# A two-layer decoder trunk: the expert stage written as a stream of 24 steps, the residual added once a token

## The chip, the core and the metric

The kernel runs on one core of a Trainium2 chip. Its engines are TensorE (PE in the profile; PEld is its loading of stationary operands), VectorE (DVE), ScalarE (ACT), GpSimd (POOL) and SyncE (SP), which here only issues transfers. The metric is the device time of one execution in microseconds.

## The reference, cut to what matters

512 tokens of width 1024 pass two layers. Each layer is a mixer (gated spatial mixing in the first, dilated attention in the second, memory attention in both), a layer norm, and an expert stage with a second layer norm:

```python
x = layer_norm(ALPHA * x + att, ln1_g, ln1_b)
expert, gate = route(x, w_router, b_router)          # 2 of 16 experts a token
ffn = sum over the token's 2 experts of
      gate * ((silu(x @ w_gate[e]) * (x @ w_up[e])) @ w_down[e])
x = layer_norm(ALPHA * x + ffn, ln2_g, ln2_b)        # LN_EPS = 1e-5
```

ALPHA is 4 to the power 1/4. The weights of an expert are three matrices of 1024 x 1024 in fp32, 12.6 MB, and each of the 2 x 16 experts is computed.

## The kernel before, in words

A product of fp32 operands is made from three matmuls: each operand is split into a high part (fp32r, made on ScalarE by a copy) and a low part (raw minus high, made on VectorE); `mm3` (L119) issues high x high, high x low and low x high. `split_to` (L115) makes the two parts, and a weight tile of 128 x 1024 is one split (L116, L117, tiles `wh` and `wl`; four `wh`, and three `wl` in layer 0 or four in layer 1, by `lows`).

`moe` (L1148) is the expert stage of a layer. `route` (L842) has given each token two experts and a rank in each; `index` and `slots` (L915, L1007) turn ranks into lists of token rows by a one-hot on VectorE (L1003) and small matmuls on TensorE, and, from expert 2 on, for two experts at a time. `gather` (L1044) fetches an expert's up to 128 rows from `hbuf` in HBM with an indirect transfer on GpSimd's queue. `turn` (L1049) transposes them on TensorE into `xh` and `xl`, and then ScalarE scales the gathered rows in place by a factor that holds ALPHA for the token's first expert and 0 for its second (L1054). `gate_up` (L1061) makes, in two halves of 512 columns, the gate and the up product (tiles `pg`, `pu`; four splits and 24 matmuls each), the silu on ScalarE, `sg` = silu x gate factor x up on VectorE (L1077), four transposes (`at`, L1080), and its parts `ah` and `al` (L1083, L1084). `down` (L1106) makes the down product (`pd`) in two halves; ScalarE copies it to `y`, GpSimd adds the scaled rows (`y <- y, xg`, L1130), and an indirect transfer scatters `y` into `ybuf` (L1131), which holds two rows a token. So the residual travels with the first expert's rows. An expert is 24 splits of weights, 144 matmuls, and 16 transposes.

The last expert isn't scattered: its rows stay on the chip (`yl`) and `last_slots` (L1087) makes a one-hot `oT` for it. `combine` (L1255) then adds, for each of the four tiles of 128 tokens, the two rows of `ybuf` (`yrows`, loaded by `load_rows`, L495), where the factor `far` blanks the row that the last expert would have filled (one ScalarE and one VectorE operation a tile), and the last expert's rows by matmuls with `oT`, and takes the norm. Its order on VectorE is written by hand as a string of steps (L575, L1316).

Weights arrive in loads of 2 MB into a ring of eight slots (`load_half`, L1139), issued by SP in one batch an expert; a load waits until the slot's last reader is done. Ahead of the experts stand `gates` (L928), `extra` (L960), `first_factors` (L1034: one-hots and small matmuls for experts 0 and 1), the split of two weight tiles, and `overflow` (L1197): every engine reads from `tabi` the number of blocks beyond 128 rows an expert and branches over a loop that does them. No such block occurs here.

The order of instructions on an engine in the expert stage is the program's scheduler's, apart from places that name an instruction to be behind (`issue_after`). `InOrder` (L58) wraps an engine so that each of its instructions is put behind the one before:

```python
with self.tc.issue_after(self.prev) if self.prev and self.strict else ExitStack():
    r = getattr(self.eng, name)(*args, **kw)
self.prev = r.ins
```

Of the kernel before, what the change touches and what calls it, by code (L numbers as in the profile page):

```python
# [38 lines left out]
SKIP = 4096  # L39
GUESS = 0xDF0259DF - (1 << 32)  # L40
# [33 lines left out]
class Trunk:  # L74
    def __init__(self, ctx, tc, a):
        self.tc, self.nc, self.a = tc, tc.nc, a
        self.lows = 3
# [5 lines left out]
        self.xbuf = tc.dram_tile([S, D], F32, name="xbuf")  # L83
        self.obuf = tc.dram_tile([2, S, 264], F32, name="obuf")
# [26 lines left out]
    def parts_tiles(self, pool, bufs):  # L111
        return (pool.tile([P, 1024], F32R, tag="wh", name="wh", bufs=bufs),
                pool.tile([P, 1024], F32R, tag="wl", name="wl", bufs=min(bufs, self.lows)))

    def split_to(self, raw, hi, lo, eng=None):  # L115
        self.hi = self.nc.scalar.activation(hi, raw, AF.Copy)  # L116
        self.sub = (eng or self.nc.vector).tensor_sub(lo, raw, hi.bitcast(F32))  # L117
# [53 lines left out]
    def rsqrt_steps(self, t, var, dve):  # L171
# [3 lines left out]
        yield dve.tensor_scalar(v, var, EPS, None, op0=OP.add)  # L175
# [11 lines left out]
    def norm_steps(self, pool, z, zn, dve, act):  # L187
# [6 lines left out]
        yield from self.rsqrt_steps(mv[:, 2:5], mv[:, 1:2], dve)  # L194
# [74 lines left out]


    def rows_to_T(self, rows, hi, lo, bank=None, order=(), act=()):

        nc = self.nc
        for b in range(2):
            x = (bank or self.tp)("xt")
            for i in range(4):
                nc.tensor.transpose(x[:, i * P:(i + 1) * P], rows[:, (4 * b + i) * P:(4 * b + i + 1) * P], self.ident)  # L277
            x3 = x.rearrange("p (a b) -> p a b", a=4)
            with ExitStack() as es:
                for ins in act:  # L280
                    es.enter_context(self.tc.issue_after(ins))
                nc.scalar.activation(hi[:, 4 * b:4 * b + 4], x3, AF.Copy)  # L282
            with ExitStack() as es:
                for ins in order:
                    es.enter_context(self.tc.issue_after(ins))
                nc.vector.tensor_sub(lo[:, 4 * b:4 * b + 4], x3, hi[:, 4 * b:4 * b + 4].bitcast(F32))


    def layer_a(self):
# [20 lines left out]
        with ExitStack() as em:  # L310
# [59 lines left out]
            for t in range(NT):  # L370
                nc.gpsimd.dma_start(self.ybuf[2 * t * P:2 * (t + 1) * P].rearrange("(p k) d -> p (k d)", k=2), zero)
# [123 lines left out]
    def load_rows(self):  # L495

        self.ys = [v[:, i * 2048:(i + 1) * 2048].rearrange("p (k d) -> p k d", k=2)
                   for v in (self.slot("yrows") for _ in range(2)) for i in range(2)]
        for t in range(NT):
            self.nc.sync.dma_start(self.ys[t], self.ybuf.rearrange("(t p k) d -> t p k d", p=P, k=2)[t])  # L500

    def layer_b(self):
# [3 lines left out]
        with ExitStack() as em:  # L506
# [72 lines left out]
            load(0)  # L579
            qT = pb.tile([P, 2, S], F32, name="qTb")  # L580
# [261 lines left out]
    def route(self, pl, lg):  # L842
# [65 lines left out]
        self.at, self.fac = [], []  # L908
        for e in range(2):
            self.index(pl, e, 1, "f", S - 1)  # L910
# [4 lines left out]
    def index(self, pool, e0, n, tag, mask=None):  # L915

        ix = self.keep(f"ix{e0}", [P, 2, n], I32)
        info = self.info if mask else self.all6
# [88 lines left out]
    def slots(self, pool, rank, info, n, ix, fac, tag, mask=None):  # L1007
# [17 lines left out]
        if fac is not None:  # L1025
            self.reduce_factors(fac, v[:, :, 2:])
# [79 lines left out]
    def down(self, act, xg, ix, i, weights, split, nodep=None, inplace=False):  # L1106
# [20 lines left out]
        if last:  # L1127
            return
# [251 lines left out]
```

## Time and profile before

| | us |
|---|---|
| median of three runs | 1726.21 (1724.07 to 1726.26) |
| the profiled execution | 1723.48 |
| its span, first to last instruction | 1721.6 |
| TensorE's mean granted clock | 0.968 |
| experts of layer 0 | from 229.1 to 810.8 |
| experts of layer 1 | from 1103.5 to 1686.8 |

Times of the trace count from the start of the span. Between the two expert stages lie the combine of layer 0 and the mixer of layer 1; behind the second lies the combine of layer 1. In a row of the trace an arrow out<-in names what is written and read, `xN` counts instructions, and a bracket [idle <-releaser] gives how long the engine had stood before and what ended that.

### The profile page before, as it was taken

What the parts mean: (1) busy time and instruction counts of PE and PEld (TensorE: products, weight loads), DVE (VectorE), ACT (ScalarE), POOL (GpSimd) and SP (SyncE); (2) the same over time, 40 slices, a digit from 0 to 9 for tenths busy, and PEclk for the clock granted to TensorE, in tenths of its full rate; (3) what the DMA queues carried; (4) which work ended last, traced back from release to release, by engine and by line L of the source; (5) the groups of instructions that cost most, each with busy time, mean ns of one, the idle gap of its engine ahead of it and who ended that gap; (6) DMA issues with size and microseconds to landing.
All of it is one profiled execution on the core that took longest, in us unless ns stands there. A gap on an engine that the chain in (4) does not pass through costs nothing. (4 is left out here: it accounts for less than half of the span.)

```text
span 1721.6 us, 21239 instructions
## 1 busy us (share of the span) xinstructions
PE 1603.4 (93%) x7608; PEld 1270.8 (74%) x7608; DVE 1441.0 (84%) x1910; ACT 1176.0 (68%) x1487; POOL 303.2 (18%) x170
## 2 busy tenths in 40 slices
PE   7999799999999999999799998499999999999994
PEld 6778577777777777777677777377777787877773
DVE  3856789999999998998735457899999999998997
ACT  3644467878888887886434434488887888888873
POOL 1201511332111211111300002211112111121002
PEclk9999889999999999999899997699999999999997
DMA  7516589999999999985422244589998999999951
GB/s 313 214 49 245 196 319 356 351 349 371 356 369 369 361 374 365 352 311 211 147 98 74 95 175 145 196 340 362 347 352 337 368 377 377 368 349 363 360 199 49
DMA packets 50739, 486.93 MB, mean 283 GB/s; under 512 B 9973, under 2 KB 10101, under 8 KB 21056
## 3 DMA queue, kind: packets, MB, share of 16 engines
q1 hardware_dynamic: 39408, 453.63, 67.8%
q0 software_dynamic: 10640, 29.75, 4.6%
q10 hardware_dynamic: 576, 2.10, 0.4%
q8 instruction: 62, 1.02, 0.2%
q14 instruction: 53, 0.43, 0.1%
HBM read 471.47 MB, written 29.39 MB: 291 GB/s over the span
## 5 line engine op out<-in xcount | busy, mean ns | idle before, releaser
L117 DVE TENSOR_TENSOR wl<-wexp,wh 128x1024 fp32r<-128x1024 f32 x768 | 945.9, 1271 | 50.1 <-ACT wh L116 30.0
L116 ACT ACTIVATE wh<-wexp 128x1024 fp32r<-128x1024 f32 x768 | 802.7, 1060 | 163.2 <-PE pg L123 73.5
L1130 POOL TENSOR_TENSOR y<-y,xg 128x1024 f32<-128x1024 f32 x30 | 92.4, 3080 | 837.9 <-ACT y L1126 837.9
L122 PE MATMUL pg<-wl,xh 128*128 128x512 f32 x512 | 205.6, 401 | 8.8 <-DVE wl L117 7.8
L122 PE MATMUL pd<-wl,ah 128*128 128x512 f32 x512 | 205.7, 402 | 5.6 <-DVE wl L117 4.6
L121 PE MATMUL pd<-wh,ah 128*128 128x512 f32 x512 | 206.5, 403 | 0.0
L123 PE MATMUL pd<-wh,al 128*128 128x512 f32 x512 | 204.4, 399 | 0.0
L123 PE MATMUL pg<-wh,xl 128*128 128x512 f32 x512 | 203.0, 396 | 0.0
L121 PE MATMUL pg<-wh,xh 128*128 128x512 f32 x512 | 202.6, 396 | 0.3 <-ACT xh L282 0.3
L122 PE MATMUL pu<-wl,xh 128*128 128x512 f32 x512 | 199.7, 390 | 1.0 <-DVE wl L117 1.0
L123 PE MATMUL pu<-wh,xl 128*128 128x512 f32 x512 | 199.5, 390 | 0.0
L121 PE MATMUL pu<-wh,xh 128*128 128x512 f32 x512 | 199.3, 389 | 0.0
L122 PEld LDWEIGHTS pg<-wl,xh 128*128 128x128 f32 x512 | 96.8, 189 | 43.5 <-DVE wl L117 24.6
L122 PEld LDWEIGHTS pd<-wl,ah 128*128 128x128 f32 x512 | 96.3, 188 | 32.2 <-DVE wl L117 12.0
L121 PEld LDWEIGHTS pd<-wh,ah 128*128 128x128 f32 x512 | 96.3, 188 | 25.3 <-ACT wh L116 5.1
L122 PEld LDWEIGHTS pu<-wl,xh 128*128 128x128 f32 x512 | 96.1, 188 | 22.3 <-DVE wl L117 2.2
L123 PEld LDWEIGHTS pd<-wh,al 128*128 128x128 f32 x512 | 96.2, 188 | 21.9 <-DVE al L1084 1.8
L121 PEld LDWEIGHTS pg<-wh,xh 128*128 128x128 f32 x512 | 96.9, 189 | 20.1 <-ACT xh L282 0.8
L121 PEld LDWEIGHTS pu<-wh,xh 128*128 128x128 f32 x512 | 96.1, 188 | 20.4
L123 PEld LDWEIGHTS pg<-wh,xl 128*128 128x128 f32 x512 | 96.6, 189 | 19.5 <-issue 0.9
L123 PEld LDWEIGHTS pu<-wh,xl 128*128 128x128 f32 x512 | 96.1, 188 | 19.9
L1046 POOL DMA_INDIRECT xg<-hbuf,ix x32 | 58.6, 1830 | 84.6 <-ACT ah L1083 67.7
(397 smaller groups left out, 2402.3 us busy)
## 6 DMA issues: line engine op xcount, KB each, us to landing
wexp<-w_moe SPq DMA_DIRECT2D x177, 2048.0 KB, 8.8
wexp<-w_moe SPq DMA_DIRECT2D x24, 1024.0 KB, 6.8
yrows<-ybuf SPq DMA_DIRECT2D x8, 1024.0 KB, 7.6
wb<-wbr SPq DMA_DIRECT2D x4, 2048.0 KB, 11.0
wexp<-w_moe POOLq DMA_DIRECT2D x3, 2048.0 KB, 10.7
ybuf<-mematt POOLq DMA_DIRECT2D x4, 1024.0 KB, 14.1
wina<-wina SPq DMA_DIRECT2D x2, 2048.0 KB, 18.7
wouta<-w_out_a SPq DMA_DIRECT2D x2, 2048.0 KB, 10.9
```

Source lines behind the costliest of these rows:

```text
L116: self.hi = self.nc.scalar.activation(hi, raw, AF.Copy)
L117: self.sub = (eng or self.nc.vector).tensor_sub(lo, raw, hi.bitcast(F32))
L121: nc.tensor.matmul(out, a[0], b[0], start=start, stop=False)
L122: nc.tensor.matmul(out, a[0], b[1], start=False, stop=False)
L123: self.mm = nc.tensor.matmul(out, a[1], b[0], start=False, stop=stop)
L1046: return self.nc.gpsimd.indirect_dma_start(out=xg, out_offset=None, in_=self.hbuf, in_offset=off, bounds_check=S - 1, oob_is_err=False)
L1130: nc.gpsimd.tensor_add(y, y, xg)
```

## The change

The expert stage is written as a stream. `mm3` takes an order; in the expert stage it is high x high, low x high, high x low, so the low part of the weights comes last. `block` goes through an expert in 24 steps, one split weight tile and six matmuls each, and calls `part` before and `at` behind each step's products; VectorE, ScalarE and TensorE are wrapped with `InOrder` for the length of the stage, so they run in the order in which the program writes. The high part is written four steps ahead of its use and the low part three (five `wh`, four `wl`). The `sg` product of a half comes ahead of the split in steps 8 and 16, its transposes behind the products of these steps, and its parts in steps 9 and 17. Index lists are made for one expert at a time in steps 10 to 13; the next rows are transposed in steps 17 to 20, and the gather of the expert after the next goes out in step 13. SP issues one load every four steps.

The residual no longer travels with the rows. The gate is divided by ALPHA and the norm's epsilon by its square, so that x is added unscaled, once a token: in the last expert's steps 10 to 17 SP fetches the four tiles of `hbuf`, and GpSimd adds to the first row of each token in `ybuf` (already loaded) first x and then the second row. `far` and its operations go, `ybuf` is zeroed for both layers (in layer B by four copies on GpSimd's queue from a zero buffer of 1 MB, `zbuf`, which layer A writes). The factors of experts 0 and 1 are made in their steps 0 to 5, behind the branch; three weight tiles are split ahead of it instead of two.

```diff
+AHEAD_H, AHEAD_L = 4, 3
+READY = 3
...
-    def mm3(self, out, a, b, start, stop):
-        nc = self.nc
-        nc.tensor.matmul(out, a[0], b[0], start=start, stop=False)
-        nc.tensor.matmul(out, a[0], b[1], start=False, stop=False)
-        self.mm = nc.tensor.matmul(out, a[1], b[0], start=False, stop=stop)
+    def mm3(self, out, a, b, start, stop, order=((0, 0), (0, 1), (1, 0))):
+        for n, (i, j) in enumerate(order):
+            self.mm = self.pe.matmul(out, a[i], b[j], start=start and n == 0, stop=stop and n == 2)
...
-            for t in range(NT):
-                nc.gpsimd.dma_start(self.ybuf[2 * t * P:2 * (t + 1) * P].rearrange("(p k) d -> p (k d)", k=2), zero)
+            for rows in [self.ybuf[2 * t * P:2 * (t + 1) * P] for t in range(NT)] + [self.zbuf]:
+                nc.gpsimd.dma_start(rows.rearrange("(p k) d -> p (k d)", k=2), zero)
...
             load(1)
             load(0)
+            for t in range(NT):
+                nc.gpsimd.dma_start(self.ybuf[2 * t * P:2 * (t + 1) * P], self.zbuf)
...
+    def block(self, pool, x, fac, part, y, at):
...
+        for c in range(24):
+            i, j = divmod(c, 4)
+            key = [("pg", 0), ("pu", 0), ("pg", 1), ("pu", 1), ("pd", 0), ("pd", 1)][i]
+            if j == 0:
+                bank[key] = self.acc(key[0])
+            if c in (8, 16):
+                times(c // 8 - 1)
+            if c == 17:
+                list(turns.pop(1))
+            if c == 20:
+                y(0, bank["pd", 0])
+            p = part(c)
+            if c in (4, 12):
+                silu(c // 8)
+            if c == 9:
+                list(turns.pop(0))
+            self.products(bank[key], x if i < 4 else a, p, j)
+            if c in (8, 16):
+                half = c // 8 - 1
+                turns[half] = self.turn(sg[half], self.tp("at"), a, half)
+                next(turns[half])
+            at(c)
+        y(1, bank["pd", 1])
...
+        self.dve, self.act, self.pe = (InOrder(tc, e, True) for e in (nc.vector, nc.scalar, nc.tensor))
...
+            if e == 0:
+                spread((0, 1, 2), index(0))
+                spread((3, 4, 5), index(1))
+            if e + 2 < NE:
+                spread((10, 12, 13), index(e + 2))
+            if not last:
+                spread((17, 18, 18, 18, 19, 19, 20), rows_in(e + 1))
+            else:
+                spread((11, 12, 13), self.last_slots(pool))
+                for t in range(NT):
+                    do(10 + t, lambda t=t: self.presum(t, 0))
+                for t in range(NT):
+                    do(14 + t, lambda t=t: self.presum(t, 1))
+
+            def get(c, e=e):
+                k = 24 * e + c
+                while len(his) < min(k + AHEAD_H + 1, 24 * NE):
+                    his.append(self.wh_tile(pool))
+                    self.hi = self.act.activation(his[-1], chunk(len(his) - 1), AF.Copy)
+                while len(los) < min(k + AHEAD_L + 1, 24 * NE):
+                    n = len(los)
+                    los.append(self.wl_tile(pool))
+                    self.sub = self.dve.tensor_sub(los[n], chunk(n), his[n].bitcast(F32))
+                return his[k], los[k]
+
+            def at(c, e=e, jobs=jobs):
+                for job in jobs.get(c, ()):
+                    job()
+                if c % 4 == 3:
+                    n = 6 * e + c // 4 + 8
+                    if n < 6 * NE:
+                        loaded.append(self.load_half(layer, *divmod(n, 6), 2 if n >= 6 * (NE - 1) else 1))
+                    elif n < 6 * NE + 4:
+                        self.tail_slot(layer, n - 6 * NE)
+
+            def y(half, bank, e=e, last=last):
+                s = slice(half * 512, (half + 1) * 512)
+                if last:
+                    self.split_to(bank, self.yl[0][:, s], self.yl[1][:, s])
+                    return
+                if half == 0:
+                    ys[e] = self.y_tile()
+                self.act.activation(ys[e][:, s], bank, AF.Copy)
+                if half:
+                    self.scatter(ys.pop(e), self.at[e], scat)
...
+    def presum(self, t, i):
+        y = self.ys[t]
+        if i == 0:
+            r = self.y_tile() if t == 2 else self.xg[t % 2 if t < 2 else 0]
+            self.nc.sync.dma_start(r, self.hbuf[t * P:(t + 1) * P, :])
+        self.nc.gpsimd.tensor_add(y[:, 0], y[:, 0], y[:, 1] if i else r)
...
             y = [self.ys[t][:, i] for i in range(2)]
-            act.activation(y[0], y[0], AF.Copy, scale=self.far[:, t, 0:1])
-            dve.scalar_tensor_tensor(y[0], y[1], self.far[:, t, 1:2], y[0], op0=OP.mult, op1=OP.add)
...
-            steps["b", t] = steps["c", t] = self.norm_steps(pool, z, y[0], dve, act)
+            steps["b", t] = steps["c", t] = self.norm_steps(pool, z, y[0], dve, act, EPS / ALPHA ** 2)
```

## Rows read from the trace of the kernel before

**Rows 1.** The page, part 1: busy us, share of span, instructions.

```profile
PE 1603.4 (93%) x7608; PEld 1270.8 (74%) x7608; DVE 1441.0 (84%) x1910; ACT 1176.0 (68%) x1487; POOL 303.2 (18%) x170
```

**Rows 2.** By stage: stretch, us, busy us by engine, clock, DMA share, GB/s.

```profile
229.00:776.00 547.00, 537.27 (x2461) 427.48 (x2462) 513.20 (x500) 446.89 (x496) 101.03 (x42) 1.00 0.91 356
812.00:1103.00 291.00, 247.20 (x1299) 194.08 (x1300) 178.62 (x464) 113.07 (x261) 45.97 (x37) 0.89 0.34 124
1434.00:1470.00 36.00, 35.95 (x163) 28.73 (x163) 33.75 (x32) 30.04 (x34) 6.17 (x3) 1.00 0.95 378
1688.00:1722.00 34.00, 12.74 (x32) 6.75 (x32) 27.16 (x65) 8.96 (x12) 10.09 (x4) 0.73 0.16 62
```

**Rows 3.** Timeline, TensorE: first products of experts (start us, us, engine, line, operation).

```profile
266.87 0.47 PE L121 MATMUL pg<-wh,xh 128*128 128x512 f32 x1
...
775.99 0.39 PE L121 MATMUL pg<-wh,xh 128*128 128x512 f32 x1
...
1140.71 0.47 PE L121 MATMUL pg<-wh,xh 128*128 128x512 f32 x1
...
1469.59 0.39 PE L121 MATMUL pg<-wh,xh 128*128 128x512 f32 x1
...
1505.04 0.40 PE L121 MATMUL pg<-wh,xh 128*128 128x512 f32 x1
...
1652.05 0.40 PE L121 MATMUL pg<-wh,xh 128*128 128x512 f32 x1
```

**Rows 4.** Waits of TensorE's weight loads, 267 to 776 us (total, times, longest).

```profile
PEld pg L122 <- DVE wl L117: 10.6, 19, 1.4
PEld at L1080 <- DVE sg L1077: 8.4, 19, 1.1
```

**Rows 5.** Groups by line, 267 to 776 us (count, busy, mean ns, idle before).

```profile
L117 DVE TENSOR_TENSOR wl<-wexp,wh 128x1024 fp32r<-128x1024 f32 x337 | 420.7, 1287 | 17.1 <-ACT wh L116 6.8 <-issue 2.7 <-PE pd L122 2.3
...
L1077 DVE SCALAR_TENSOR_TENSOR sg<-sg,fac,pu 128x512 f32<-128x512 f32 x28 | 20.8, 742 | 10.7 <-PE pu L123 10.7
L1084 DVE TENSOR_TENSOR al<-at,ah 128x512 fp32r<-128x512 f32 x28 | 19.1, 683 | 0.5 <-ACT ah L1083 0.5
```

**Rows 6.** All operations on the low parts, whole span (min/median/max ns).

```profile
L117 DVE TENSOR_TENSOR wl<-wexp,wh x768: 1208/1218/3433, 221.4 to 1683.6; 128x1024 fp32r<-128x1024 f32 x192
```

**Rows 7.** Timeline of VectorE around an add of GpSimd, layer 0.

```profile
303.36 2.35 DVE L117 TENSOR_TENSOR wl<-wexp,wh 128x1024 fp32r<-128x1024 f32 x2
...
306.23 7.97 DVE L117 TENSOR_TENSOR wl<-wexp,wh 128x1024 fp32r<-128x1024 f32 x5
```

**Rows 8.** Timeline of GpSimd in the same stretch.

```profile
305.09 6.89 POOL L1130 TENSOR_TENSOR y<-y,xg 128x1024 f32<-128x1024 f32 x1 [29.82 <-ACT y L1126]
```

**Rows 9.** All operations on the expert's rows (min/median/max ns).

```profile
L1130 POOL TENSOR_TENSOR y<-y,xg x30: 2507/2636/6890, 267.5 to 1652.9; 128x1024 f32<-128x1024 f32 x30
```

**Rows 10.** Groups by line, 1140 to 1652 us: the one-hot.

```profile
L1003 DVE TENSOR_TENSOR so<-rk,slot 128x512 bf16<-128x512 f32 x11 | 7.5, 685 | 0.0
```

**Rows 11.** Timeline of VectorE ahead of layer 1's experts: the overflow count.

```profile
1092.09 0.14 DVE L970 CAST tabi<-tab 1x1 int32<-1x1 f32 x1
```

**Rows 12.** Timeline of TensorE ahead of layer 1's experts.

```profile
1095.13 0.36 PE L1041 MATMUL fac<-all,so 128*128 128x4 bf16 x8 [5.07 <-DVE all L955]
1101.66 1.94 PE L277 MATMUL xt<-ident,xg 128*128 128x128 f32 x8 [6.17 <-PEq L1201]
```

**Rows 13.** Timeline of TensorE ahead of layer 0's experts.

```profile
227.75 1.07 PE L277 MATMUL xt<-ident,xg 128*128 128x128 f32 x8 [1.92 <-DVEq L1201]
```

**Rows 14.** Transfers in 40 slices of 740 to 812 us, mean GB/s.

```profile
GB/s 396 378 118 378 407 369 364 382 401 309 428 428 405 410 396 46 93 198 0 0 0 0 0 87 36 305 432 428 428 428 391 346 410 423 437 428 437 36 0 0
```

**Rows 15.** Operations with the factor far, both layers (min/median/max ns).

```profile
L67 DVE SCALAR_TENSOR_TENSOR yrows<-yrows,far x8: 1237/1280/2468, 811.4 to 1698.4; 128x1024 f32<-128x1024 f32 x8
```

**Rows 16.** Waits in the first 80 us.

```profile
ACT wh L116 <- DMA wina<-wina: 2.2, 3, 1.8
```

**Rows 17.** Waits of SP's queue, 229 to 776 us (total, times, longest).

```profile
SPq L1144 <- DVE wl L117: 498.5, 88, 9.7
```

More of the change, by code (lines that the diff above doesn't have):

```diff
@@ L493, in load_branch @@
         self.nc.sync.dma_start(qk, self.a["wbr"][:, c:c + 4096])
[L495 to L500, printed above, removed]
     def layer_b(self):
@@ L1087, in last_slots, with scatter @@
-    def last_slots(self, pool, layer):
-        nc = self.nc
-        self.hgb = self.slot("ln2")
-        self.load_ln2(layer, 0)
-        y2 = self.slot("ylast").bitcast(F32R)
-        self.yl = y2[:, :D], y2[:, D:2 * D]
-        self.oT = y2[:, 2 * D:2 * D + S]
-        so = self.one_hot(pool, self.rk[:, :, NE - 1:])
-        x = self.tp("oT")
-        for t in range(NT):
-            nc.tensor.matmul(x[:, t * P:(t + 1) * P], so[:, t], self.identb, start=True, stop=True)
-        nc.scalar.activation(self.oT, x, AF.Copy)
+    def scatter(self, y, ix, nodep):
+        st = self.nc.gpsimd.indirect_dma_start(out=self.ybuf, out_offset=bass.IndirectOffsetOnAxis(ap=ix[:, 1], axis=0),
+                                               in_=y, in_offset=None, bounds_check=2 * S - 1, oob_is_err=False)
+        for other in nodep:
+            self.tc.declare_no_dep(st.ins, other.ins, reason="rows of other tokens")
+        nodep.append(st)
@@ L1146, in load_half, with wh_tile, wl_tile, turn @@
         return t
+    def wh_tile(self, pool):
+        return pool.tile([P, 1024], F32R, tag="wh", name="wh", bufs=AHEAD_H + 1)
+    def wl_tile(self, pool):
+        return pool.tile([P, 1024], F32R, tag="wl", name="wl", bufs=AHEAD_L + 1)
+    def turn(self, src, bank, parts, half):
+        for q in range(4):
+            self.pe.transpose(bank[:, q * P:(q + 1) * P], src[:, q * P:(q + 1) * P], self.ident)
+        s = slice(4 * half, 4 * half + 4)
+        x3 = bank.rearrange("p (a b) -> p a b", a=4)
+        yield
+        self.act.activation(parts[0][:, s], x3, AF.Copy)
+        yield
+        self.dve.tensor_sub(parts[1][:, s], x3, parts[0][:, s].bitcast(F32))
@@ new lines, in y_tile, with two, products @@
+    def y_tile(self):
+        return self.px.tile([P, D], F32, tag="y", name="y", bufs=1)
+    def two(self, pool, names):
+        return [pool.tile([P, KT, P], F32R, tag=n, name=n, bufs=1) for n in names]
+    def products(self, bank, a, part, j):
+        h, l = part
+        for q in range(2):
+            kt = 2 * j + q
+            c = slice(q * 512, (q + 1) * 512)
+            self.mm3(bank, (a[0][:, kt], a[1][:, kt]), (h[:, c], l[:, c]), start=(kt == 0), stop=(kt == 7),
+                     order=((0, 0), (1, 0), (0, 1)))
@@ L1151, in moe @@
             self.px = px
-            self.xg = [pool.tile([P, D], F32, name=f"xg{i}") for i in range(2)]
-            first = [self.gather(*self.at[e], self.xg[e]) for e in range(2)]
+            self.xg = [px.tile([P, D], F32, name=f"xg{i}") for i in range(2)]
+            first = [self.gather(self.at[e], self.xg[e]) for e in range(2)]
             scat = []
-            split = self.ahead(pool)
             loaded = list(self.early)
```

388 lines of the change are left out of this document (167 added, 221 removed).

## The prediction, made before the changed kernel ran

> **What bounds the kernel now.** I read the page's busy shares first [rows 1]. TensorE is busy 93% of the span and VectorE 84%, but these are means over stages with different limits, so the table by stage comes next [rows 2]. From 229 to 776 us, fifteen experts of the first layer, TensorE is busy 537 of 547 us, VectorE 513, and the transfer engines 0.91. Overlapping matmuls are counted busy even where a short wait lies between them, so a busy share cannot say how much is left to win. For that I take the period: the start of the first product of an expert [rows 3]. Experts 1 to 14 of layer 0 take 775.99 - 266.87 = 509.1 us, 36.37 each; those of layer 1 take 1652.05 - 1140.71 = 511.3 us, 36.52 each. The best one, from 1469.59 to 1505.04, takes 35.45, with the same products. So about 1 us of an expert is waiting, and the rest is TensorE's own work.
>
> What TensorE waits for stands in the waits of its weight loads [rows 4]: 10.6 us for low parts (wl) in the gate product and 8.4 us for the gated activation (sg), both made on VectorE. These loads run ahead of the matmuls, so 19.0 us in 14 experts, 1.36 each, is an upper bound of the stall. Why is VectorE late? One split costs 1.218 us in the median but 1.287 in the mean of this stretch, and the longest took 3.43 [rows 5, 6]. Two that follow each other need 2.35 us, so the pitch is 2.35 - 1.22 = 1.13 us; five, from 306.23, took 7.97 where that pitch gives 5.74 [rows 7]. In that stretch GpSimd's residual add ran, and took 6.89 us instead of its median 2.64 [rows 8, 9]. So the two engines stop each other: GpSimd got in only when VectorE had a hole, and then VectorE stood about 2.2 us.
>
> **The change part by part.** *Stream and chain.* Removed in each expert are the residual add on GpSimd and the scaling of the gathered rows on ScalarE. VectorE regains 24 x (1.287 - 1.218) = 1.66 us. It keeps 24 x 1.13 = 27.1 us of splits, two sg (0.74 each), two al and two xl of one shape (0.68 each) [rows 5], one one-hot (0.69) [rows 10] and four small index operations of the kind that take 0.14 us [rows 11]: 32.6 us of an expert. TensorE's products and transposes stay as they are. What moves is the order: each step first issues the high part four steps ahead and the low part three ahead, and the two products with the high part come before the one with the low part, so a late low part has two matmuls more. The two sg products come one step ahead of the transposes that read them. I take 35.4 us an expert, the best row of before, in which one residual add still ran. Ends: 36.37 - 1.36 = 35.0 if all waits of [rows 4] go, and 36.4 if none does. Term: 509.1 + 511.3 - 28 x 35.4 = **-29.2 us**.
>
> *First experts.* Three steps are split ahead instead of two, two one-hots (0.7 each) move in behind them. **-1 us** for both layers, between 0 and -2.
>
> *Before the stage.* The factor matmuls (L1041) go behind the branch. In layer 1 they waited 5.07 us for the gates, and only then did TensorE reach its branch, where it spent 6.17 us more [rows 12]; the count that the branch reads was written at 1092.09 [rows 11]. TensorE can now start that wait some 3 us earlier, and VectorE, which has two one-hots and one split less, is through by then. In layer 0 the wait behind the branch is 1.92 us [rows 13], of which I take 1. **-4 us**, between 0 and -5.
>
> *The residual, once a token.* Eight GpSimd adds of 2.5 us follow in the last expert, after four 1 MB reads of ybuf and four 0.5 MB reads of hbuf on SP. On that queue the reads wait for expert 14's scatter, as they did before, and 6.3 MB take 15 us at the 428 GB/s that the transfers reach there [rows 14]; so the first add starts past the middle of the expert, an estimate. VectorE is then asked for at most half of its 24 splits, has 35.4 - 32.6 = 2.8 us free and no xl to make (1.4 more), and is three steps ahead. About three adds fall before its last split, 3 x 2.2 = 6.6 us, less than these together. I take +1 us a layer, **+2 us**; ends 0 and +20 (first rival).
>
> *Tail.* The four far operations a layer, 1.28 us each on VectorE [rows 15], and its add of the last rows (0.7, al's shape) go; the norms behind them are VectorE's chain (27.2 of 34 us [rows 2]). That is 5.8 us a layer. The last adds of GpSimd now fall on it, and VectorE's short two-input operations can stand behind each, 2.2 us at most. I take one, so 3.6 a layer, **-7 us**; ends 0 and -12.
>
> *Start.* A fifth 1 MB is zeroed. Transfers are saturated there, and ScalarE waits for first-layer weights 2.2 us in all [rows 16]. **+1 us**; ends 0 and 2.5 (1.05 MB at the 428 GB/s of [rows 14]).
>
> *At nothing.* The four copies that zero ybuf again lie in layer B, where the transfer engines are 0.34 busy [rows 2]; they stand on GpSimd's queue ahead of the attention's small transfers, and without that cover 8.4 MB would cost some 20 us of transfer. Gathers and scatters keep their place and their queue. The weight loads move from one batch an expert to one every four steps, but SP already waits for a free slot 498.5 us in this stretch [rows 17], so the slot sets them still; each slot still comes free at its last split. The factor 1/alpha is one small VectorE operation.
>
> Sum: -29.2 - 1 - 4 + 2 - 7 + 1 = -38 us. On the profiled execution's 1723.48 us (2.7 below the median of the three runs) that is 1685.3; I write **1686**.
>
> **The rivals.** *GpSimd and VectorE alternate.* In [rows 7, 8] neither gives way during an instruction. If GpSimd finds a hole after every split of the last expert, each of the some seven splits still to come waits for an add: 7 x (2.5 + 1.2) = 26 us in place of 7 x 1.4 = 10. Three steps of lead, 4 us, are taken off, and the last expert ends 12 us late in each layer, where I took 1. Time: 1686 + 2 x 11 = 1708. Against it: in [rows 7, 8] four operations in a row went ahead of the add, so a late VectorE keeps GpSimd out and recovers. Beside that stands a rule of the Trainium skill, page "SBUF — State Buffer", section "Who interferes with whom": a VectorE instruction with two SBUF inputs and a GpSimd instruction that reads SBUF exclude each other for the whole instruction, and the one that issues first wins. The trace agrees with the lock (6.89 us against 2.64); by the rule alone, with both always ready, the alternation is what comes.
>
> *Only the adds' share goes.* If the scheduler already issued nearly this order, the stalls not tied to the adds stay: 14 us of the 29 are left, and the time is 1701.
>
> *The weight stream is the bound.* If 36.4 us an expert were the rate of the transfers, nothing of the 29 would come: 1715. Against it: SP waits for slots, not slots for SP [rows 17], and 378 GB/s were moved in the best expert's neighbour [rows 2], 428 elsewhere [rows 14]. The Trainium skill speaks for it: "SBUF — State Buffer", section "A bandwidth-pool intuition that's wrong", gives about 358 GB/s from HBM to a core. The six 2 MB loads of an expert would need 35.1 us by that, with its rows over 36; the measured 378 GB/s is above the figure, so I keep the rival small.
>
> *Slower: the order itself stalls VectorE.* sg must now wait in order for its product, and the splits behind it wait too; in the old order such waits already cost 10.7 us in 14 experts [rows 5]. If both sg and both al idle VectorE 1.3 us each, its 32.6 us become 37.8, and it, not TensorE, sets the expert. The change is lost from 35.4 + 38/28 = 36.8 us on; at 37.5 the time is 1686 + 28 x 2.1 = 1745. Against it: three steps of lead (3 x 1.4 us) cover any one such wait.
>
> **How the numbers follow.** Chances: forecast 0.66, alternation 0.12, adds' share only 0.08, stream 0.05 (0.01 of it within 0.2%), slower 0.07, and 0.02 for no change at all; a last expert without stall and 35.0 us an expert lie inside the forecast at 1668. The range 1664 to 1712 holds the forecast with its ends, the alternation and the adds' share. A measurement of this kernel tells about 0.2% from no change. Faster by more than that 0.90, within it 0.03, slower 0.07.
>
> **What would show it.** Right: the period of experts 1 to 14 near 35.4 in both layers, no wl above 1.3 us outside the last expert, weight loads that wait for sg gone, and the first transposes of layer 1 some 3 us nearer to the count. Adds in the last expert should be stretched like the 6.89 one, and the last of them end in the tail. Wrong: a period above 36; wl of 2.5 us and more in every step of the last expert; SP waiting for nothing while TensorE waits for weights.

## The result, and the profile after

The changed kernel takes 1694.5 us (median of four runs, 1693.6 to 1697.5) against 1725.8: a ratio of 0.9823, 95% interval 0.9806 to 0.9841. It is faster, as forecast, and lies in the range; the forecast itself, 1686, is 8.5 us too low. The profiled execution took 1693.88 us, its span is 1692.0. Of all executions behind the numbers below one is left out as slow: 8856.8 us, of the kernel with gated adds. The page's busy shares hardly moved [rows 1]:

```profile
PE 1585.1 (94%) x7608; PEld 1279.8 (76%) x7608; DVE 1409.3 (83%) x1934; ACT 1136.5 (67%) x1447; POOL 228.2 (13%) x159
```

The period moved. The first products of experts 0 and 1, of expert 15, and the same in layer 1, in the timeline of TensorE:

```profile
232.57 0.80 PE L68 MATMUL pg<-wh,xh 128*128 128x512 f32 x1
...
269.44 0.40 PE L68 MATMUL pg<-wh,xh 128*128 128x512 f32 x1
...
759.06 0.40 PE L68 MATMUL pg<-wh,xh 128*128 128x512 f32 x1
...
1091.27 0.77 PE L68 MATMUL pg<-wh,xh 128*128 128x512 f32 x1
...
1128.76 0.40 PE L68 MATMUL pg<-wh,xh 128*128 128x512 f32 x1
...
1618.37 0.40 PE L68 MATMUL pg<-wh,xh 128*128 128x512 f32 x1
```

Experts 1 to 14 take 489.62 us in layer 0 and 489.61 in layer 1, 34.97 each, where they took 36.37 and 36.52 [rows 3]. From the table by stage of the changed kernel, with the columns of [rows 2]:

```profile
233.00:759.00 526.00, 526.00 (x2464) 429.79 (x2464) 497.08 (x526) 432.90 (x481) 36.86 (x28) 1.00 0.95 374
```

Waits of TensorE's weight loads in the changed kernel, 269 to 759 us (the count and the longest behind the total):

```profile
PEld L68 <- issue: 3.4, 13, 0.3
```

Its groups by line in the same stretch:

```profile
L68 DVE TENSOR_TENSOR wl<-wexp,wh 128x1024 fp32r<-128x1024 f32 x337 | 403.1, 1220 | 16.8 <-ACT wh L68 4.2 <-PE pd L68 2.4 <-issue 0.2
...
L68 DVE SCALAR_TENSOR_TENSOR sg<-sg,fac,pu 128x512 f32<-128x512 f32 x28 | 20.9, 747 | 1.7
```

All its operations on the low parts:

```profile
L68 DVE TENSOR_TENSOR wl<-wexp,wh x762: 1211/1219/3425, 234.3 to 1658.7; 128x1024 fp32r<-128x1024 f32 x191
```

Waits of its SP queue in that stretch:

```profile
SPq L1021 <- DVE wl L68: 440.1, 82, 6.7
```

TensorE is busy in all 526.00 of 526 us. No weight load waits for a split or for sg any more; VectorE's wait ahead of sg (10.7 us in [rows 5]) is 1.7. So 34.97 us is the matmuls' own time. Transfers move 374 GB/s in this stretch, and SP's queue still waits for slots for 440.1 of 490 us, so the stream of weights is not the bound. The Trainium skill gives less ("SBUF — State Buffer", section "A bandwidth-pool intuition that's wrong": about 358 GB/s from HBM to a core); by that an expert would have stayed above 35.1 us, and the measured 374 decides.

Where the span went, stretch by stretch (us, before to after; the last product of a layer ends at 810.79 and 1686.78 before, 795.22 and 1662.79 after):

| stretch | before | after | change |
|---|---|---|---|
| start to first product of layer 0 | 229.11 | 232.57 | +3.5 |
| expert 0, layers 0 and 1 | 37.76, 37.23 | 36.87, 37.49 | -0.6 |
| experts 1 to 14, both layers | 509.12 + 511.34 | 489.62 + 489.61 | -41.2 |
| expert 15 of layer 0 | 34.80 | 36.16 | +1.4 |
| from there to the first product of layer 1 | 292.69 | 296.05 | +3.4 |
| expert 15 of layer 1 | 34.73 | 44.42 | +9.7 |
| tail | 34.87 | 29.20 | -5.7 |
| sum (span) | 1721.65 | 1692.00 | -29.7 |

The stream gave 41 us and 12 went elsewhere. The largest loss is expert 15 of layer 1, read in four views of the changed kernel.

GpSimd's timeline:

```profile
1638.11 2.40 POOL L1249 TENSOR_TENSOR yrows<-yrows,xg 128x1024 f32<-128x1024 f32 x1 [17.40 <-DMA xg<-hbuf]
1640.59 3.23 POOL L1249 TENSOR_TENSOR yrows<-yrows 128x1024 f32<-128x1024 f32 x1
1643.78 3.34 POOL L1249 TENSOR_TENSOR yrows<-yrows,xg 128x1024 f32<-128x1024 f32 x1
...
1660.52 3.23 POOL L1249 TENSOR_TENSOR yrows<-yrows 128x1024 f32<-128x1024 f32 x1
```

VectorE's timeline, of the same us:

```profile
1638.47 6.44 DVE L68 TENSOR_TENSOR wl<-wexp,wh 128x1024 fp32r<-128x1024 f32 x2 [0.24 <-issue]
...
1648.73 9.48 DVE L68 TENSOR_TENSOR wl<-wexp,wh 128x1024 fp32r<-128x1024 f32 x3
```

TensorE's waits, 1618 to 1664 us:

```profile
PE pd L68 <- DVE wl L68: 3.3, 2, 1.6
PE at L68 <- DVE sg L68: 3.1, 1, 3.1
```

The expert in slices, with the columns of [rows 2]:

```profile
1618.00:1638.00 20.00, 20.00 (x95) 16.37 (x94) 18.79 (x18) 16.88 (x20) 1.27 (x1) 1.00 0.71 288
...
1643.00:1648.00 5.00, 2.38 (x8) 2.09 (x9) 5.00 (x3) 1.23 (x2) 4.92 (x3) 0.66 0.06 25
1648.00:1653.00 5.00, 5.00 (x17) 3.91 (x16) 5.00 (x4) 2.44 (x3) 5.00 (x2) 0.66 0.00 0
```

From the second on, the eight adds follow each other at 3.2 to 3.5 us, which is one add (2.40) and a little less than one split (1.22), and two splits take 6.44 us and three 9.48: the engines take turns. TensorE waits 6.4 us. Then there is a second price: in the ten us from 1643 on, in which its wait of 3.1 us ends, the mean granted clock is 0.66, between the levels of 1.2 and 2.4 GHz. From 1646.4 to 1651.2 us products follow each other at 0.43 us instead of 0.23, which makes some 2.4 us more. Two of them in TensorE's timeline:

```profile
1648.24 0.63 PE L68 MATMUL pd<-wh,al 128*128 128x512 f32 x1
1648.67 0.63 PE L68 MATMUL pd<-wl,ah 128*128 128x512 f32 x1
```

Behind the two waits of 1.6 us in the same expert the clock is 1.00.

In layer 0 the same eight adds come later, and the combine suffers instead. GpSimd's timeline, 760 to 808 us, the first and last of four copies and of eight adds:

```profile
769.09 0.60 POOL L556 DMA_DIRECT2D ybuf<-zbuf  x1 [7.68 <-DMA yrows<-ybuf]
...
785.05 0.49 POOL L556 DMA_DIRECT2D ybuf<-zbuf  x1 [7.94 <-DMA yrows<-ybuf]
787.07 2.48 POOL L1249 TENSOR_TENSOR yrows<-yrows,xg 128x1024 f32<-128x1024 f32 x1 [1.53 <-DMA xg<-hbuf]
...
805.76 2.36 POOL L1249 TENSOR_TENSOR yrows<-yrows 128x1024 f32<-128x1024 f32 x1
```

VectorE's timeline behind the last product, 795 to 807 us:

```profile
805.72 1.29 DVE L68 BATCH_NORM_STATS2 bnst<-z 128x6 f32<-128x512 f32 x2 [9.13 <-POOL yrows L1249]
```

The four copies that zero ybuf stand ahead of the adds in GpSimd's queue. The adds begin at 787.07, 8 us before the last product ends; five of them begin behind it, and the norm's first operation waits until the seventh is done, at 805.68. That one is the last to read a buffer of the gathered rows, whose memory the combine takes over (read from the code; it was not tried alone, but the run with gated adds below, whose statistics have memory of their own, agrees). The first transposes of layer B come 26.0 us after the last product, before the change they came 17.7 us after it.

Ahead of layer 0's experts the gather is late; TensorE waits 5.20 us for it, where it waited 1.92 [rows 13]. Ahead of layer 1 the way from the count to the first transposes shrank: 9.57 us before [rows 11, 12], now 5.89. Layer 0, GpSimd's timeline, 205 to 231 us:

```profile
225.32 1.10 POOL L1001 DMA_INDIRECT xg<-hbuf,ix  x1 [16.76 <-ACT kT L221]
```

The same in the kernel before:

```profile
216.35 1.30 POOL L1046 DMA_INDIRECT xg<-hbuf,ix  x1 [8.22 <-DVE ix L1022]
```

TensorE's timeline, 225 to 233 us:

```profile
230.75 1.94 PE L68 MATMUL xt<-ident,xg 128*128 128x128 f32 x8 [5.20 <-DMA xg<-hbuf,ix]
```

Layer 1, VectorE's timeline:

```profile
1083.51 0.14 DVE L935 CAST tabi<-tab 1x1 int32<-1x1 f32 x1
```

Layer 1, TensorE's timeline:

```profile
1089.40 1.94 PE L68 MATMUL xt<-ident,xg 128*128 128x128 f32 x8 [6.99 <-DVEq L1255]
```

### The profile page after: what moved, and what is told of

Its sections match the earlier page's. It is cut to its first block, busy times and chain, and to the rows that moved or that the text cites. A ratio compares the mean times of both kernels' runs of the same rounds, so it can differ in the third digit from the quotient of the medians.

```text
span 1692.0 us, 21506 instructions
## 1 busy us (share of the span) xinstructions
PE 1585.1 (94%) x7608; PEld 1279.8 (76%) x7608; DVE 1409.3 (83%) x1934; ACT 1136.5 (67%) x1447; POOL 228.2 (13%) x159
## 5 line engine op out<-in xcount | busy, mean ns | idle before, releaser
L68 DVE TENSOR_TENSOR wl<-wexp,wh 128x1024 fp32r<-128x1024 f32 x762 | 928.1, 1242 | 38.1 <-ACT wh L68 9.4
L68 PE MATMUL pd<-wh,ah 128*128 128x512 f32 x512 | 210.5, 411 | 0.0
L68 PE MATMUL pg<-wl,xh 128*128 128x512 f32 x512 | 200.4, 391 | 0.0
L1001 POOL DMA_INDIRECT xg<-hbuf,ix x32 | 42.0, 1313 | 566.1 <-PE pu L68 482.1
L1005 POOL DMA_INDIRECT ybuf<-y,ix x30 | 38.5, 1283 | 449.4 <-ACT y L68 449.4
## 6 DMA issues: line engine op xcount, KB each, us to landing
wouta<-w_out_a SPq DMA_DIRECT2D x2, 2048.0 KB, 10.7
```

Of the source, the lines that this page charges most:

```text
L1001: return self.nc.gpsimd.indirect_dma_start(out=xg, out_offset=None, in_=self.hbuf, in_offset=off, bounds_check=S - 1, oob_is_err=False)
L1005: st = self.nc.gpsimd.indirect_dma_start(out=self.ybuf, out_offset=bass.IndirectOffsetOnAxis(ap=ix[:, 1], axis=0), in_=y, in_offset=None, ...
```

## Experiments

The time of the kernel before, run beside each, is 1722 to 1725 us. All kernels but the first start from the changed one. "Period" is the mean of experts 1 to 14. "Behind" and "ahead" are places on an engine's queue.

### What gave the 41 us: the adds that left, or the order?

**The kernel before, without the adds:**

```diff
         if not inplace:
-            nc.gpsimd.tensor_add(y, y, xg)
```

> The kernel before without GpSimd's add of the gathered rows to y in each expert; the output leaves the residual out, everything else stays. Theory A (the adds, which hold VectorE up, are the stall): the period of experts 1 to 14 falls from 36.37 and 36.52 us to 35.3 or less, the mean split (wl) to 1.22 us, and the time to about 1726 - 28 x 1.2 = 1692 us. Theory B (the scheduler's order is the stall, the adds only lengthen splits that had time): the period stays at 36.0 or above and the time at 1712 us or above.

Measured, in one execution: 1700.8 us; the period is 35.55 and 35.67 us, and no split exceeds 1.228. Between the two theories: of 1.47 us an expert the adds' leaving gives 0.83. What stays is uneven. Experts 1 to 10 take 35.2 on the mean in layer 0, experts 11 to 14 take 36.4. VectorE's waits of this run in those last four, 621 to 766 us:

```profile
DVE sg L1077 <- PE pu L123: 11.8, 8, 1.7
```

In the ten before, this wait totals 0.3 us; and the 10.7 us of [rows 5] are the same wait. So the scheduler's order put sg so early in the last experts that VectorE stood in front of it, up to 1.7 us each time, with the splits behind.

**The stream, with one add an expert put back:**

```diff
                 if half:
+                    nc.gpsimd.tensor_add(ys[e], ys[e], self.xg[(e + 1) % 2])
                     self.scatter(ys.pop(e), self.at[e], scat)
```

> The changed kernel with one GpSimd add of 128 x 1024 to y put back in each expert, ahead of its scatter (rows of the next expert are added, so the output isn't the reference's; the residual adds in the last expert stay). Theory A (an add costs what VectorE stands): the period goes from 34.97 us to 35.8 or more, and the time to 1718 us or more. Theory B (the stream's lead of three low parts and the low part's place at the end cover one add an expert): the period stays within 35.2 us and the time within 1701 us, with splits of 3 us beside each add all the same.

Measured, in one execution: period 35.15 us, 1701.7 us in all. By the period theory B holds: in the stream an add costs 0.18 us, in the old order 0.83. (One split of 3.05 us stands beside each add all the same.) The time is 0.7 us over what B named. In the traces the 28 experts are 5.0 us longer than in the changed kernel and the stretch between the layers 7.5 (303.6 us instead of 296.0), while the two last experts are 4.8 us shorter.

**The same with the old order of the three matmuls:**

```diff
-                     order=((0, 0), (1, 0), (0, 1)))
+                     order=((0, 0), (0, 1), (1, 0)))
```

> The run e2_stream_with_adds with the old order of the three matmuls (high x high, high x low, low x high, so that the low part is wanted second and not last). Theory A (the lead of three low parts covers the adds, the place of the low part adds nothing): the period stays at 35.15 us. Theory B (the two matmuls of delay are what covers them): 35.4 us or more.

Measured, in one execution: period 35.00 us, 1696.7 us in all. Neither figure was named, but B falls: placing the low part last covers nothing here, and without it an add costs 0.03. What covers is among what is left of the stream, the lead of three low parts and the chain; no run varied the lead. It is not the number of `wl` tiles alone: in layer 1 the kernel before had four, as the changed one has, and there the adds cost 0.86 us an expert (36.52 with them, 35.67 without).

**The stream without the chain:**

```diff
-        self.dve, self.act, self.pe = (InOrder(tc, e, True) for e in (nc.vector, nc.scalar, nc.tensor))
+        self.dve, self.act, self.pe = (InOrder(tc, e, False) for e in (nc.vector, nc.scalar, nc.tensor))
```

> The changed kernel with the order of VectorE, ScalarE and TensorE in the expert stage left to the scheduler (the wrapper no longer puts each instruction behind the one before; the 24 steps and the lead of four and three stay). Theory A (the chain is what keeps the splits in step): the period of experts 1 to 14 goes from 34.97 us to 35.5 or more, and the time to 1709 us or more. Theory B (the lead and the place of the low part do it, the chain only writes down what the scheduler does anyway): the period stays within 35.1 us and the time within 0.2% of 1694.5 us.

Measured: 1741.0 us, 1.0113 times the kernel before (1.0082 to 1.0143). The period shows why a mean would mislead: experts 1 to 9 take 35.1 us without any chain, experts 10 to 14 take 38.9, 41.4, 40.9, 38.5 and 37.5 in layer 0; in layer 1 expert 10 takes 35.2 and the next four 40.6, 42.9, 38.5 and 37.4. VectorE's waits of this run in those five, 584 to 782 us:

```profile
DVE sg L68 <- PE pu L68: 15.2, 4, 4.4
DVE wl L68 <- issue: 7.3, 3, 3.3
DVE al L68 <- ACT ah L68: 6.5, 2, 3.3
```

The longest is the wait of the kernel before, for sg, again, now up to 4.4 us. It is not the whole: these five experts are 22.6 us longer than with the chain, TensorE waits 13.8 us in them, and its largest wait is for gathered rows:

```profile
PE xt L68 <- DMA xg<-hbuf,ix: 4.4, 2, 2.4
```

Nine experts keep their time without the chain; the chain is what keeps it to the end of the stage. Why the scheduler's order goes off just there was not tried.

### What cost expert 15 and the combine: the residual adds?

**Without the eight adds** (the line with `gpsimd.tensor_add` in `presum` is deleted):

> The changed kernel without the eight residual adds a layer (all their reads stay; the output leaves the residual and the second row of each token out). Theory A (in layer 1 the adds alternate with VectorE's splits and stretch the last expert; in layer 0 they end late and hold the combine up): the last expert takes 34.8 us in both layers instead of 36.2 and 44.4, the first transposes of layer B come 8 us earlier after the last product, and the time is 1694.5 - 1.4 - 9.6 - 8 = 1675 us. Theory B (the last expert waits for transfers or for its own order): it stays at 42 us or more in layer 1, and the time is 1685 us or more.

Measured: 1673.7 us (ratio 0.9706, 0.9678 to 0.9734). Theory A holds in every part: expert 15 takes 34.45 us in both layers and the first transposes of layer B come 15.3 us after the last product instead of 26.0. (At the first product of layer 1, 6.1 us of these 10.7 are left.) The adds cost 21 us by the medians, 18.6 by the two traces. This kernel's first and last product of expert 15 in layer 1:

```profile
1609.68 0.40 PE L68 MATMUL pg<-wh,xh 128*128 128x512 f32 x1
...
1643.73 0.40 PE L68 MATMUL pd<-wl,ah 128*128 128x512 f32 x1
```

**The copies behind the adds** (`self.pre` is the last add):

```diff
-            for t in range(NT):
-                nc.gpsimd.dma_start(self.ybuf[2 * t * P:2 * (t + 1) * P], self.zbuf)
+            with tc.issue_after(self.pre.ins):
+                for t in range(NT):
+                    nc.gpsimd.dma_start(self.ybuf[2 * t * P:2 * (t + 1) * P], self.zbuf)
```

> The changed kernel with the four copies that zero ybuf put behind the last residual add of layer 0 on GpSimd's queue (nothing left out). Theory A (the copies stood ahead of the adds and took their transfers' time, and only so was layer 0 spared): the adds of layer 0 start some 8 us earlier after the last scatter, as in layer 1, alternate with the splits and stretch the last expert of layer 0 from 36.2 us to 42 or more; the combine behind it starts its norm right away and gains 5 to 9 us back; the time stays within 1690 to 1699 us. Theory B (the last expert of layer 0 was short for another reason): it stays at 36 us, and the time falls by the earlier end of the adds to 1687 us or less.

Measured: 1691.5 us (0.9815, 0.9799 to 0.9831). Theory A: the adds of layer 0 begin at 777.85, while the last product ends at 803.97, and expert 15 takes 44.40 us, as in layer 1. From the last product of layer 0 to the first of layer 1, 11.1 us are gained back. GpSimd's timeline of this run, the first add:

```profile
777.85 3.85 POOL L1250 TENSOR_TENSOR yrows<-yrows,xg 128x1024 f32<-128x1024 f32 x1 [15.93 <-DMA xg<-hbuf]
```

**The adds begun behind the splits:**

```diff
                     self.split_to(bank, self.yl[0][:, s], self.yl[1][:, s])
+                    if half == 0:
+                        v = self.yl[1][:, 0:1].bitcast(F32)
+                        self.pre = nc.gpsimd.tensor_add(self.keep("gate", [P, 1]), v, v)
...
+            with self.tc.issue_after(self.pre.ins):
+                self.pre = self.nc.gpsimd.tensor_add(y[:, 0], y[:, 0], r)
```

> The changed kernel with its residual adds on GpSimd, but begun only when the first half of the last expert's rows is split (one add of a single column, which reads that split, stands ahead of them in GpSimd's queue); two of the x tiles lie in free parts of the ring, the norm's statistics in memory of their own, and the four copies that zero ybuf stand behind the adds (nothing left out). Theory A (the loss is the overlap of the adds with the last expert's splits, and in layer 0 the pool that the combine waits for): the last expert takes 35.5 us or less in both layers, the combine of layer 0 starts its norm within 7 us of the last product, the tail of layer 1 is 1 to 3 us longer than 29.2, and the time is 1676 to 1680 us. Theory B (the adds cost the same wherever they stand, since the combine then waits for them): what the last expert gains the combine and the tail give back, and the time is 1688 us or more.

Measured: 1698.9 us (0.9854, 0.9834 to 0.9875). My theory fell. Expert 15 does take 34.49 us in both layers, but the tail of layer 1 grew from 29.2 to 39.6 us. GpSimd's timeline of this run, first and last add of layer 1:

```profile
1654.26 2.40 POOL L1258 TENSOR_TENSOR yrows<-yrows,xg 128x1024 f32<-128x1024 f32 x1
...
1670.96 2.35 POOL L1258 TENSOR_TENSOR yrows<-yrows 128x1024 f32<-128x1024 f32 x1
```

VectorE's timeline in the same stretch:

```profile
1663.76 9.95 DVE L68 SCALAR_TENSOR_TENSOR bnmv<-bnmv 128x1 f32<-128x1 f32 x7
```

Seven operations on one column take 9.95 us; the same seven take 1.5 us in the changed kernel, where the adds are over (1667.19 to 1668.70). They have two operands in SBUF, and in these ten us the adds follow each other without a gap; four of the seven take 2.2 to 2.4 us each, as long as one add, the other three 0.16. The waiting moved from the splits to the norm.

In layer 0 another cost came up. VectorE's timeline of this run behind the last product (793.55):

```profile
797.82 1.30 DVE L68 BATCH_NORM_STATS2 bnst<-z 128x6 f32<-128x512 f32 x2 [2.91 <-PE z L68]
...
811.07 0.23 DVE L462 TENSOR_SCALAR rel_i<-rel_i 128x129 int32<-128x129 int32 x1 [11.71 <-POOL rel_i L461]
```

With memory of its own for the statistics the norm begins while GpSimd still adds. But the next operations on VectorE's queue need an index tile of layer B (`rel_i`) that GpSimd makes behind the adds, and VectorE stands 11.71 us; 302.3 us lie between the layers instead of 296.0.

**The residual on TensorE:**

```diff
                     pe.matmul(z[half], self.ident, y[0][:, s], start=True, stop=False)
+                    pe.matmul(z[half], self.ident, y[1][:, s], start=False, stop=False)
+                    pe.matmul(z[half], self.ident, self.xr[t][:, s], start=False, stop=False)
```

> The changed kernel with no residual adds on GpSimd: the combine adds the second row and x on TensorE, by four more products with the identity a tile of tokens (16 a layer), and the norm's statistics lie in memory of their own (nothing left out). Theory A (the adds' cost is the lock and their late end, and TensorE has room in the combine): the last expert takes 34.5 us in both layers, the combine is as short as without the adds, and the time is 1677 us, within 3 us of the run that leaves them out. Theory B (TensorE, at half clock in the combine, becomes its bound): 16 x 0.43 = 6.9 us a layer come back, and the time is 1686 us or more.

Measured: 1694.6 us (0.9825, 0.9809 to 0.9842). Theory B, for a reason I had priced wrong. Expert 15 takes 34.48 us, but the tail takes 37.7. The identity products in the tail, groups by line of the changed kernel:

```profile
L68 PE MATMUL z<-yrows,ident 128*128 128x512 f32 x16 | 7.5, 592 | 0.0
```

This kernel's groups:

```profile
L68 PE MATMUL z<-yrows,ident 128*128 128x512 f32 x32 | 15.0, 592 | 0.0
...
L68 PE MATMUL z<-xg,ident 128*128 128x512 f32 x8 | 4.1, 592 | 0.0
```

Its tail from 1657 to 1682 us, with the columns of [rows 2]:

```profile
1657.00:1682.00 25.00, 24.72 (x66) 12.12 (x64) 9.77 (x42) 4.83 (x7) 6.34 (x3) 1.00 0.06 22
```

With four more of `ln` and four of `ylast` there are 48 records instead of 16, two for each fp32 product, at a pitch of 0.43 us: 32 x 0.43 = 13.8 us of TensorE a layer, not 6.9. The tail is 8.5 us longer. Nor is the clock low there, as I had thought: it is granted in full (1.00). The Trainium skill has the price ("FP8 and Floating Point Precision", section "TensorE Precision Notes": four passes for true fp32), and the trace agrees: 0.86 us a product against 0.23 for one of the split kind.

**The work shared out:** GpSimd adds only the second rows, TensorE adds x.

```diff
+        self.pre = self.nc.gpsimd.tensor_add(y[:, 0], y[:, 0], y[:, 1])
...
+                    pe.matmul(z[half], self.ident, self.xr[t][:, s], start=False, stop=False)
```

> The residual's work shared out (nothing left out): GpSimd adds only the second row of each token, four adds a layer that need no reads of x and so begin some 10 us earlier in the last expert; TensorE adds x with two more identity products a tile; statistics in memory of their own, the four copies behind the adds, the gathered rows' buffers moved as in e6_early_gather. Theory A (the cost goes by the number of adds that meet the splits, and the earlier ones leave VectorE time to recover): the last expert takes 37.5 us or less in both layers, the tail 33 us or less, the time is 1684 us or less. Theory B (each part comes back at its new place, as in e7_residual_pe and e9_gated_adds): 1689 us or more, no better than e8_all_three.

Measured: 1693.9 us (0.9821, 0.9805 to 0.9836): theory B. With half the adds, expert 15 still takes 43.88 and 43.22 us. TensorE's waits of this run in layer 1's:

```profile
PE oT L68 <- DVE so L68: 3.8, 1, 3.8
```

Slices of the same expert:

```profile
1637.00:1642.00 5.00, 1.21 (x4) 0.67 (x4) 5.00 (x5) 1.42 (x2) 2.42 (x1) 0.81 0.01 4
1642.00:1647.00 5.00, 4.70 (x15) 3.80 (x15) 3.74 (x4) 1.65 (x2) 0.00 (x0) 0.51 0.00 0
```

The four adds lie between 1627.0 and 1639.4 and use up the lead at once. Then the chain turns against the kernel: the one-hot for the last rows (so) stands behind the stretched splits on VectorE, the transposes oT stand behind so on TensorE, and oT, with all products behind it, waits 3.84 us; the five us from 1642 on run at a clock of 0.51.

### The gather

**The gathered rows' buffers where they were:**

```diff
-        a = self.two(pool, ("ah", "al"))
+        a = self.two(self.px, ("ah",)) + self.two(pool, ("al",))
...
-            self.xg = [px.tile([P, D], F32, name=f"xg{i}") for i in range(2)]
+            self.xg = [pool.tile([P, D], F32, name=f"xg{i}") for i in range(2)]
```

> The changed kernel with the two buffers of gathered rows in the memory where the kernel before had them, behind a part of the activations (nothing left out). Theory A (in layer 0 the first gather waited until TensorE had read the split weights of layer A that lay in its new buffer): it is issued at 216 to 217 us instead of 225.3, the idle time of TensorE ahead of the first transposes falls from 5.2 us to about 2, and the time falls by 3 us to 1691.5. Theory B (the gather waits for the memory products whatever its buffer): it stays at 225 us and the time at 1694.5.

Measured: 1694.7 us (0.9826, 0.9809 to 0.9842). The mechanism is right: the first gather is issued at 215.96 and the experts begin at 227.54 instead of 232.57, 5 us earlier. GpSimd's timeline of this run:

```profile
215.96 1.29 POOL L1001 DMA_INDIRECT xg<-hbuf,ix  x1 [8.22 <-DVE ix L985]
```

The time doesn't show it: from the last product of layer 0 to the first of layer 1 this run takes 302.3 us instead of 296.0. The 34 us from 22 us behind the last product on, with the columns of [rows 2]. The changed kernel:

```profile
817.20:851.20 34.00, 22.57 (x135) 20.79 (x136) 25.73 (x52) 15.00 (x27) 12.19 (x5) 0.73 0.52 186
```

This run:

```profile
812.70:846.70 34.00, 22.59 (x120) 21.09 (x121) 25.57 (x52) 13.31 (x24) 12.26 (x5) 0.62 0.52 186
```

The granted clock is 0.62 instead of 0.73 with the same waits of TensorE. What sets it apart stays open. Five other runs have 302 to 304 us there, so no gain of a few us ahead of that stage can be read from the total.

**All three** (residual on TensorE, buffers moved, copies placed behind the query products of layer B):

> The residual on TensorE, the gather's buffers moved and the four copies behind the query products of layer B, together (nothing left out). Theory A (the three losses are separate): 1677 - 3 = 1674 us, or 1 to 2 less as the copies no longer collide with the loads of the last expert. Theory B (they overlap, or the copies now delay the attention's transfers): 1678 us or more.

Measured: 1688.7 us (0.9796, 0.9780 to 0.9812), the fastest kernel here that computes everything, 5 to 6 us below the changed one, though the two intervals overlap by a little. Theory B in size. Against the changed kernel's trace it has 3.9 us less ahead of the experts and 11.7 less in the two last experts, but 8.5 more in the tail and 1.7 more between the layers: what the residual on TensorE gives in the last experts it mostly takes back, as above. The copies did not move: they are issued from 765.40 on, since the place that I named is on ScalarE and orders nothing on GpSimd.

**The gated adds with the buffers moved:**

> The run before this one with the buffers of the gathered rows also moved, as in e6_early_gather (nothing left out). Theory A (the front gains 5 us as there, and what that run lost behind it was the clock of its combine): 1671 to 1676 us. Theory B (the buffers' place costs layer B what it gives at the front): the same time as the run before this one, within 2 us.

Measured: 1698.3 us (0.9849, 0.9830 to 0.9868). Theory B: the experts begin at 226.93, and 302.2 us lie between the layers; the total is that of the run without the move, and the traces show where 3.2 of the 4.9 us at the front went: into expert 0 of the two layers (38.75 and 37.82 us, there 36.79 and 36.57).

## Why the prediction was right, and where its terms were wrong

- **Experts 1 to 14**, forecast -29.2 us, measured -41.2. The mechanism (waits of TensorE for a late VectorE go) is shown; the term was mis-sized by choosing 35.4, the best row of before, over the end of 35.0 that [rows 4] gave. The best row still had an add in it. The bound from the waits, 36.37 - 1.36, was the better estimate: 34.97.
- **Whose share.** "Only the adds' share goes" had 14 us of 29 left for the adds. Shown: taking the adds out gives 0.83 of 1.47 us, the new order with the adds still there 1.29; so some 0.65 us of an expert is cured by either.
- **First experts**, -1 forecast, -0.6 measured. **Start**, +1 forecast; TensorE reaches layer 0's rank products 0.4 us later (212.47 before, 212.90).
- **Before the stage**, forecast -4. Layer 1 gave it: from the end of the rank products to the first product 15.3 us before, 10.8 now. Layer 0 lost 3.0 instead of gaining 1, so the term came to -1.5. The failing step is "Gathers and scatters keep their place and their queue". They do, but their buffers moved, by the code into memory that layer A's splits had used, and the first gather went out 9 us later (216.35 before), when the memory products were done. The experiment with the buffers moved back shows it.
- **The residual in the last expert**, forecast +2, measured +11.1. The failing step is "VectorE is then asked for at most half of its 24 splits, has 35.4 - 32.6 = 2.8 us free ... and is three steps ahead". I let a late VectorE keep GpSimd out, from [rows 7, 8], where four operations passed one waiting add; here none passed, each add got its turn behind one split. Why the two differ no run shows. My first rival, the alternation, is what came in layer 1: 12 us forecast, 9.7 measured. The rule that I set beside it (the Trainium skill, "SBUF — State Buffer", "Who interferes with whom": exclusive for the whole instruction, whoever issues first wins) is borne out as to the lock by the pitch of 3.2 to 3.5 us. As to the order it is not borne out by [rows 7, 8]: the add begun at 305.09 let splits begun from 306.23 on go first. Layer 0 was spared by accident, by the copies.
- **At nothing: the copies.** I hid them in layer B. They stood in the last expert, ahead of the adds; so the combine of layer 0 waited, and its tail term (-3.6) came out as +9.3: from the last product to layer B's first key product 45.1 us before, 54.4 after. In layer 1 the tail gave -5.7 against -3.6.
- **The sum** (-38) was 8 us off the profiled -29.6 because two errors met: the experts gave 12 us more than forecast, and all the rest together cost 12 us where it was to give 9. One figure is a slip: 35.0 us an expert and a last expert without stall make 1673 by the prediction's own terms, not 1668.
- **The rival on the other side** (in-order waits for sg) did not come: with the chain VectorE's wait ahead of sg is 1.7 us in 14 experts. It came where the chain was taken off (37.4 to 42.9 us in the experts just before the last one, with other waits beside it).
- **The signs.** As named, no split outside the last expert exceeds 1.3 us, and the first transposes of layer 1 are 3.7 us nearer to the count. The adds were not stretched like the 6.89 one (3.4 us at most), and splits of 2.5 us and more, named as a sign of being wrong, came in seven steps of layer 1's last expert.

## What to carry to other kernels

A bulk addition on GpSimd beside VectorE's two-operand work cost something at each place where the two met: in the last experts 16 adds of 2.4 us, 38 us in all, took 21 us, and four ways of moving them again gave back at most 3 of these. Spread singly over a stream with a lead it cost 0.03 to 0.18 us an expert; and the row-by-row residual inside the stream (with its ScalarE scaling, which was not tried) is where I would look next. Where buffers move, look what their memory held before: a transfer can wait for its last reader.

## What I had not expected of the hardware

- A wait of TensorE cost twice in two places: with one of 3.1 us the granted clock was 0.66 over ten us, with one of 3.84 us in the shared-out run 0.51 over five, and products then stood 0.43 us apart instead of 0.23.
- An fp32 product with the identity stands in the trace as two records, 0.43 us apart at full clock; a product of split parts is one record of 0.23.
- Seven one-column operations took 9.95 us beside GpSimd's adds: four of them stood for as long as one whole add, so the lock went by instructions, not by bytes.
